# Weight splits, idle matmuls and one right operand of the up projection: a layer's first stage re-ordered, and the third operand's low part made by a DMA

## The chip, the core and the metric

The kernel runs on one NeuronCore of one Trainium2 chip. The metric is the device time of one execution in microseconds. An execution that is profiled leaves a page and a trace; others are only timed. The engines are called as in the profile: PE (TensorE matmuls), PEld (its weight loads), DVE (VectorE), ACT (ScalarE), POOL (GpSimd), SP (SyncE, which here only issues DMAs). PE, DVE and ACT each run their instructions strictly in order.

## The reference

One layer of a hybrid trunk for 1024 tokens and 1024 channels, in float32:

```python
h = rms_norm(x, g_mix)
z = einsum("bsd,de->bse", h, w_in) + b_in        # 1024 x 1024 by 1024 x 7168
va, ga, xb, gb, sa, sb = split(z)
# conv branch of va, ga; RG-LRU branch of xb, gb; both gated and merged to m
x = x + einsum("bsd,de->bse", m, w_o)
h = rms_norm(x, g_mlp)
f = square(relu(einsum("bsd,df->bsf", h, w_1)))  # the up projection, 1024 x 4096
x = x + einsum("bsf,fd->bsd", f, w_2)
return rms_norm(x, g_final)
```

## The kernel before, in words

**Products.** Every float32 operand is split into a high part, rounded to the type that PE multiplies in one pass, and a low part, the rest. A product is the sum of three matmuls: high by high, high by low and low by high. The high part is a copy by ScalarE. The low part is made in one of two ways: `low` (L703) and `split` (L51) subtract the high part from the source on VectorE; `split_dma` (L64 to L68) has ScalarE copy the source with its sign turned (L66), and a DMA issued by POOL adds the source onto that copy (L67, `accum_op=ALU.add`); the high part follows (L68). In the names of tiles, `h` and `l` at the end stand for high and low.

**First stage.** The tokens are taken in two halves of 512. Row sums of squares come from `x_square` (L186), alternating between VectorE and ScalarE in the first half and on ScalarE in the second. `x_root` (L199) makes of them 1/rms by a square root on ScalarE and Newton's step on VectorE (L95 to L105), and puts it on four diagonals (L208 by VectorE, L210 by ScalarE). `x_spread` (L212) multiplies these by a matrix of ones (L217), so that every partition holds the factor of every token: the PSUM tile `rb`. `x_scaled` (L219) multiplies a column block c of the transposed x by it on VectorE (L221) and takes the high part `xh` on ScalarE (L222); `x_low` (L224) takes the low part `xl` on VectorE (L226). There are eight column blocks. They meet the first three column chunks of `w_in` (`N0 = 3`, PSUM tiles z16 to z18). `first_w` (L233) splits a chunk's weight by `split_dma`; `first_z` (L242, matmuls on L245) does its high part by `xh` and `xl`; `late_z` (L248, L250) its low part by `xh`. `half` (L315) lays out one half of the tokens: for each c the scaling of block c, whatever `beside` adds, the low part of block c-1, and the matmuls that this allows; a chunk joins at the c in `joins`. Ahead of the first products stand idle matmuls (`idle_mm`, L303 to L305): ones by the identity, 16 and then 6, whose result nobody reads. They write the second half of the tile `rb`. All this stands in a block `manual_schedule` (L292), in which the order of PE, DVE and ACT is that of the text; POOL and SP, and the rest of the kernel outside such blocks, are ordered by a scheduler that estimates times. From the fourth chunk on, `zchunk` (L353) does each chunk with `mm3` (matmuls on L92).

**DMAs of the first stage.** SP loads, in this order: four row tiles of x, weight 0, two pieces of the transposed x, weight 1, a piece, weight 2, a piece, four more row tiles, four pieces of the second half, then the weights of later chunks.

**Up projection.** h by w_1 is done in blocks of two by two, by a scheme with seven products p = 1 to 7 instead of eight, for each of 16 tiles i of two chunks of 128 columns. `h2_sum` (L733) makes the right operands (sums of blocks `hq` in `ht`; for p = 3 the block itself), `h2_part` and `h2_parts` (L711, L743) split them into `b{p}h` and `b{p}l` with `low`. `up_load` loads a tile's weights, `up_lhs` (L762) makes the left operand o of (i, p): sums `s` on VectorE (L773 to L777), the high part on ScalarE (L785), the low part on VectorE (L704). `up_step` (L805) does 12 matmuls (`up_mm`, L794) and reads them off. Four PSUM banks a, b, c, d serve a tile: p = 1, 2 write a, 6 writes b, 5 and then 3 write c, 7 and then 4 write d. The sum of p = 5 is read from c by VectorE (L821) before p = 3 goes on in the same bank, likewise d (L823) between p = 7 and p = 4. L819 reads b. In the traces the banks of tile 0 are f0a to f0d.

The first four tiles (`AHEAD = 4`) are done in part while the right operands are still being made. That is a second block `manual_schedule` (L880 to L920); behind it a loop (L1011) does the rest of the list `seq`, which holds (0, 6), (0, 5), (0, 7), (0, 3), (0, 4), (1, 6) and so on. It prepares left operands `look = 5` steps ahead, before the step's matmuls. In the block stand, at the end: the left operand of (0, 7), the steps (0, 6) and (0, 5), both halves of the right operands 3 and 4 with `h2_parts`, and the left operands of (0, 3) and (0, 4). The step (0, 7) is the loop's first.

Of the kernel before, what the change touches and what calls it, by code (L numbers as in the profile page):

```python
# [9 lines left out]
F32 = mybir.dt.float32  # L10
F32R = mybir.dt.float32r
# [21 lines left out]
def trunk_kernel(ctx: ExitStack, tc: tile.TileContext, x, xt_in, vecs, w_in, w_a_out, w_b_out,  # L33
# [145 lines left out]
    for t in range(4, 8):  # L179
        load_x(t)  # L180

# [17 lines left out]
    def x_root(hf):  # L199

        ss, v, s, t, r = (rs_x[hf][:, i, :] for i in range(5))
        nc.vector.tensor_scalar(v, ss, 1.0 / D, EPS, ALU.mult, ALU.add)
        newton_rstd(r, v, s, t)
        rb["d"] = rd = T(f"rd{hf}")
        for i in range(4):
            d = rd[:, i * P:(i + 1) * P]
            if i % 2 == 0:
                nc.vector.tensor_scalar(d, ident, r[:, i:i + 1], None, ALU.mult)  # L208
            else:
                nc.scalar.activation(d, ident, AF.Copy, scale=r[:, i:i + 1])  # L210
# [22 lines left out]
    def first_w(i):  # L233
        if i < 2:
            wh, wl = split_w(raw0[i], [P, 8, P], f"w{i}")
        else:
            wh, wl = (T(f"w{i}_{n}", F32R).rearrange("p (k c) -> p k c", c=P) for n in "hl")
            split_dma(raw0[i], wh, wl)
        w0.append((wh, wl))
        z0.append(PS(f"z{16 + i}"))  # L240

    def first_z(i, hf, ks):  # L242
        for k in ks:
            for n, a in enumerate((xh, xl)):
                nc.tensor.matmul(z0[i][:, HALVES[hf]], w0[i][0][:, k, :], a[k][:, HALVES[hf]],  # L245
                                 start=k == 0 and n == 0, stop=False)

    def late_z(i, hf, ks=range(8)):  # L248
        for k in ks:
            nc.tensor.matmul(z0[i][:, HALVES[hf]], w0[i][1][:, k, :], xh[k][:, HALVES[hf]],  # L250
                             start=False, stop=k == 7)
# [40 lines left out]
    with tc.manual_schedule(engines={mybir.EngineType.Activation, mybir.EngineType.DVE,  # L292
# [7 lines left out]
        rb["tile"] = PS("rb", "ps2")  # L300
        nc.tensor.matmul(rb["tile"][:, 0:1], ones, rs_x[0][:, 0, 1:2], start=True, stop=True)

        def idle_mm(n):  # L303
            for _ in range(n):
                nc.tensor.matmul(rb["tile"][:, HS:HS + P], ones, ident, start=True, stop=True)  # L305

        idle_mm(16)
        x_root(0)
        x_spread(0)
        idle_mm(6)  # L310
        first_w(0)
        for c2 in range(4):
            load_xc(1, c2)

        def half(hf, beside, joins):  # L315


            seen = [0] * N0
            for c in range(9):
                if c < 8:  # L320
                    x_scaled(hf, c)
                beside(c)
                if c:
                    x_low(hf, c - 1)
                    for i in range(N0):
                        if c >= joins[i]:
                            first_z(i, hf, range(seen[i], c))
# [12 lines left out]
        late_z(1, 0)  # L340
        x_spread(1)
        late_z(2, 0)
        half(1, lambda c: None, (1, 1, 1))
        late_z(1, 1)
        late_z(2, 1)
# [400 lines left out]

    NP = DFF // P // 2
# [132 lines left out]
    with tc.manual_schedule(engines={mybir.EngineType.Activation, mybir.EngineType.DVE,  # L880
# [31 lines left out]
        h2_sum(3, 1)  # L912
        up_step(0, 6, up_ps)
        h2_parts(3)
# [4 lines left out]
        h2_parts(4)  # L919
        up_lhs(0, 4)  # L920
    KC = 2
# [90 lines left out]
    for n in range(2 * AHEAD + 2, len(seq)):  # L1012
# [251 lines left out]
```

## Time and profile before

| what | value |
|---|---|
| median of 3 timed runs | 1625.59 us (1624.93 to 1626.24) |
| the profiled execution: time, span of its trace | 1623.46 us, 1621.6 us |
| PE busy | 1601.3 us, 99% of the span |
| PE waits, first stage, on its first products | 1.50, 0.22, 0.53 and 0.30 us |
| PE waits, up projection, 1024 to 1034 us | 0.10, 0.80 and 1.13 us |
| granted clock of TensorE | 1.00, but 0.50 from 18.6 to 25.4 us |

Times in the views are microseconds from the first instruction of the trace. A row of a timeline gives start, duration, engine, line, operation, output and inputs by the program's names with shapes, the number of instructions merged into the row, and in brackets the engine's idle time before it with the line that ended it. Matmuls overlap, so that a row's duration (0.39 us) is longer than the distance from one to the next; a PE that shows as busy is not on that account at its peak. The rows of the view of stretches give busy time and count of PE, PEld, DVE, ACT and POOL, then the clock (1.00 is full), the mean busy share of the 16 DMA engines and what they moved in GB/s. "To landing" is the time from a DMA's issue to its last byte.

### The profile page before, as it was taken

To read this page: it belongs to the slowest core of one execution; us is meant where nothing else is said; L and a number is where in the kernel's file an instruction comes from. 1 tells how busy PE (TensorE), PEld (TensorE's weight loads), DVE (VectorE), ACT (ScalarE), POOL (GpSimd) and SP (SyncE) were. 2 spreads that over 40 slices of the span, in tenths; PEclk is the share of its full clock that TensorE was granted. 3 is DMA by queue.
4 is the path that set the end of the run, shared out by engine and by line. 5 is a ranking of instruction groups with operands and counts; after the bars stand their busy time and mean duration, and the time that the engine had idled before them with its cause. 6 is when DMAs were issued, how large, how long until landed. Compare 5 with 4: busy or idle time off the path is not lost.

```text
span 1621.6 us, 18723 instructions
## 1 busy us (share of the span) xinstructions
PE 1601.3 (99%) x7070; PEld 1314.9 (81%) x7070; DVE 1094.7 (68%) x1319; ACT 931.2 (57%) x1185; POOL 179.8 (11%) x244
## 2 busy tenths in 40 slices
PE   7999999999999999999999999999999999999997
PEld 6888888888888888888788888788888888888886
DVE  4699999998989836611412146965555457888898
ACT  5579898999972347722522335654444466555552
POOL 1111111111210100010211100000000001111110
PEclk9999999999999999999999999999999999999999
DMA  9456676667755544464755641433322579889862
GB/s 317 100 116 159 133 152 147 158 146 167 173 129 127 131 98 97 91 201 98 172 146 123 182 156 65 171 116 116 117 104 104 184 231 233 213 216 228 213 130 104
DMA packets 81513, 245.90 MB, mean 152 GB/s; under 512 B 9568, under 2 KB 11104, under 8 KB 81424
## 3 DMA queue, kind: packets, MB, share of 16 engines
q0 software_dynamic: 29392, 97.24, 29.6%
q1 hardware_dynamic: 51888, 147.22, 27.5%
q8 instruction: 55, 0.90, 0.2%
q14 instruction: 34, 0.28, 0.1%
q10 hardware_dynamic: 144, 0.26, 0.0%
HBM read 123.05 MB, written 33.55 MB: 97 GB/s over the span
## 4 chain that ended last, share of the span: by engine, by line
PE 96%; DVE 1%; ACT 1%; issue 1%; DMA 0%; SPq 0%; DVEq 0%; ACTq 0%
PE z L92 35%; PE d L1048 14%; PE yb L92 8%; PE ya L92 5%; PE o L656 3%; PE e L1163 2%; PE keep L1048 2%; PE o L92 2%; PE z L245 1%; PE rg L419 1%; PE rg L421 1%; PE rg L420 1%; PE o L680 1%; PE z L250 1%; PE tr_m L728 0%
## 5 line engine op out<-in xcount | busy, mean ns | idle before, releaser
L492 DVE SCALAR_TENSOR_TENSOR y<-u,vec,y 128x1024 f32<-128x1024 f32 x240 | 307.2, 1280 | 15.8 <-ACT y L488 10.7
L92 PE MATMUL z<-xh,win_h 128*128 128x512 f32 x848 | 262.8, 391 | 0.0
L92 PE MATMUL z<-xl,win_h 128*128 128x512 f32 x848 | 261.8, 390 | 0.0
L92 PE MATMUL z<-xh,win_l 128*128 128x512 f32 x848 | 200.9, 389 | 0.0
L92 PEld LDWEIGHTS z<-xh,win_h 128*128 128x128 f32 x848 | 159.3, 188 | 35.8 <-issue 1.7
L92 PEld LDWEIGHTS z<-xl,win_h 128*128 128x128 f32 x848 | 159.2, 188 | 33.7 <-issue 0.2
L92 PEld LDWEIGHTS z<-xh,win_l 128*128 128x128 f32 x848 | 159.2, 188 | 33.0
L1060 DVE TENSOR_TENSOR acc<-acc,d 128x1024 f32<-128x1024 f32 x72 | 87.8, 1219 | 33.3 <-PE d L1048 32.6
L68 ACT ACTIVATE win_h<-win_raw 128x1024 fp32r<-128x1024 f32 x53 | 55.9, 1056 | 89.7 <-PE z L92 79.3
L67 POOL DMA_DIRECT2D win_l<-win_raw x53 | 46.6, 880 | 338.8 <-ACT win_l L66 313.1
L66 ACT ACTIVATE win_l<-win_raw 128x1024 fp32r<-128x1024 f32 x53 | 55.5, 1050 | 5.7 <-PE z L92 5.7
L619 DVE TENSOR_TENSOR sb<-yb,sb 128x1024 f32<-128x1024 f32 x8 | 9.8, 1224 | 72.3 <-PE yb L92 72.3
L785 ACT ACTIVATE o<-s 128x512 fp32r<-128x512 f32 x64 | 38.1, 621 | 34.7 <-DVE s L777 29.6
L595 DVE TENSOR_TENSOR m<-ya,sa 128x1024 f32<-128x1024 f32 x8 | 9.8, 1225 | 68.8 <-PE ya L92 68.8
L785 ACT ACTIVATE o<-w_raw 128x512 fp32r<-128x512 f32 x40 | 25.0, 624 | 50.9 <-DVE o L704 50.8
L574 DVE TENSOR_TENSOR v<-v,ge 128x512 f32<-128x512 f32 x24 | 16.4, 689 | 47.7 <-ACT ge L572 47.7
L381 DVE SCALAR_TENSOR_TENSOR v<-xb,vec,v 128x1023 f32<-128x1023 f32 (+2 forms) x36 | 45.3, 1271 | 1.2 <-ACT v L376 1.1
L67 POOL DMA_DIRECT2D db_1l<-wr x7 | 6.1, 872 | 356.9 <-ACT db_1l L66 334.4
L688 DVE TENSOR_TENSOR x<-xr,o 128x1024 f32<-128x1024 f32 x8 | 9.6, 1219 | 51.9 <-PE o L656 37.7
L704 DVE TENSOR_TENSOR o<-s,o 128x512 fp32r<-128x512 f32 x64 | 42.5, 684 | 2.9 <-ACT o L785 2.8
L118 ACT ACTIVATE xn<-x 128x1024 f32<-128x1024 f32 x8 | 8.4, 1057 | 58.5 <-DVE x L688 53.4
L92 PE MATMUL ya<-suh,wa_h 128*128 128x512 f32 x128 | 39.4, 389 | 0.0
(1101 smaller groups left out, 3859.0 us busy)
## 6 DMA issues: line engine op xcount, KB each, us to landing
win_raw<-in_w_in_dram SPq DMA_DIRECT2D x53, 512.0 KB, 4.5
win_l<-win_raw POOLq DMA_DIRECT2D x53, 512.0 KB, 4.6
fr<-fd SPq DMA_DIRECT2D x32, 512.0 KB, 5.2
wr<-in_w_dram SPq DMA_DIRECT2D x32, 512.0 KB, 5.9
w_raw<-in_w_dram SPq DMA_DIRECT2D x31, 512.0 KB, 3.4
gates<-s POOLq DMA_DIRECT2D x32, 256.0 KB, 4.3
fd<-fa SPq DMA_DIRECT2D x16, 512.0 KB, 3.1
fd<-fb SPq DMA_DIRECT2D x16, 512.0 KB, 3.0
```

The lines of the kernel that those rows point to most:

```text
L66: nc.scalar.activation(l, src, AF.Copy, scale=-1.0)
L67: nc.gpsimd.dma_start(l, src, accum_op=ALU.add)
L68: nc.scalar.activation(h, src, AF.Copy)
L92: nc.tensor.matmul(ps[:, HALVES[hf]], a, b[hf], start=i == 0, stop=i == len(todo) - 1)
L381: nc.vector.scalar_tensor_tensor(v[:, d:S], a[:, 0:S - d], cbw_c[:, w * 12 + t:w * 12 + t + 1], v[:, d:S], ALU.mult, ALU.add)
L492: nc.vector.scalar_tensor_tensor(acc, u[:, w:w + S], caw[:, w * 8 + j:w * 8 + j + 1], acc, ALU.mult, ALU.add)
L656: nc.tensor.matmul(ps[:, HALVES[hf]], tok(a, k, t), wo[k][b][:, HALVES[hf]], start=k == 0 and b == 0 and n == 0, stop=k == 7 and b == 1)
L704: tt(l, src, h.bitcast(F32), ALU.subtract)
L785: nc.scalar.activation(o[:, 0], src, AF.Copy)
L1048: nc.tensor.matmul(o, a, b, start=n == 0 and (p != 1 or g == 0), stop=n == len(todo) - 1, skip_group_check=p == 1 and g > 0)
L1060: tt(acc[p, q2], acc[p, q2], ps, ALU.add)
L1163: nc.tensor.matmul(o, a, b, start=n == 0, stop=n == len(todo) - 1)
```

## The change

In the first stage:

- The idle matmuls write a PSUM tile `spare` of their own instead of the second half of `rb`.
- `first_w` comes in parts. The high part of weight 0 is copied by ScalarE inside `x_root(0)`, ahead of the diagonals. The low parts of weights 0 and 1 are subtracted by VectorE; weight 2 keeps the copy with turned sign and the accumulating DMA. The low part of weight 0 stands ahead of the first scaling, that of weight 1 ahead of the low part of column block 2.
- Chunk 0 takes its three products of a column block at once, high by low in between, with one idle matmul before and one after the product with the first low part. Chunks 1 and 2 join one column block earlier; their products of the weight's low part stay at the end of a half.
- The four loads of the second half's transposed x are written further up.

In the up projection:

- Right operand 3 is split by `split_dma` instead of by VectorE, ahead of the step (0, 6).
- The step (0, 7) comes into the hand-ordered block, ahead of the subtraction for the second half of right operand 4; the left operand of (0, 4) comes between the two halves of right operand 4.

```diff
+    for c2 in range(4):
+        load_xc(1, c2)
...
-    def x_root(hf):
+    def x_root(hf, beside=lambda: None):
...
         newton_rstd(r, v, s, t)
+        beside()
...
-    def first_w(i):
+    def first_w(i, part):
+        if part == "h":
...
+            nc.scalar.activation(wh, raw0[i], AF.Copy)
+        elif part == "l":
+            nc.vector.tensor_tensor(w0[i][1], raw0[i], w0[i][0].bitcast(F32), ALU.subtract)
         else:
-            split_dma(raw0[i], wh, wl)
+            nc.scalar.activation(w0[i][1], raw0[i], AF.Copy, scale=-1.0)
+            nc.gpsimd.dma_start(w0[i][1], raw0[i], accum_op=ALU.add)
...
+        spare = PS("spare")
...
-                nc.tensor.matmul(rb["tile"][:, HS:HS + P], ones, ident, start=True, stop=True)
+                nc.tensor.matmul(spare[:, 0:P], ones, ident, start=True, stop=True)
         idle_mm(16)
-        x_root(0)
+        x_root(0, lambda: first_w(0, "h"))
+        rb["tile"] = PS("rb", "ps2")
         x_spread(0)
+        first_w(0, "l")
         idle_mm(6)
-        first_w(0)
...
                 if c:
+                    first_z(0, hf, c - 1, "hh")
+                    first_z(0, hf, c - 1, "lh")
+                    if c in idle:
+                        idle_mm(idle[c])
                     x_low(hf, c - 1)
-                    for i in range(N0):
-                        if c >= joins[i]:
-                            first_z(i, hf, range(seen[i], c))
-                            seen[i] = c
-                    if c > 4:
-                        late_z(0, hf, (2 * c - 10, 2 * c - 9))
+                    first_z(0, hf, c - 1, "hl")
+                    for i in range(1, N0):
+                        while joins[i] <= c and seen[i] < c:
+                            first_z(i, hf, seen[i], "hh")
+                            first_z(i, hf, seen[i], "hl")
+                            seen[i] += 1
+                    if c in idle:
+                        idle_mm(idle[c])
         def beside(c):
             if c in (1, 2):
-                first_w(c)
-            elif 4 < c < 9:
+                first_w(c, "h")
+            elif c == 3:
+                first_w(1, "l")
+                first_w(2, "dma")
+            if 4 < c < 9:
                 x_square(c - 1, nc.scalar)
-        half(0, beside, (1, 3, 4))
+        half(0, beside, (1, 2, 3), {1: 1})
...
+    def h2_parts_dma(p):
+        for c2 in range(2):
+            bh[p][c2], bl[p][c2] = T(f"b{p}h{c2}", F32R), T(f"b{p}l{c2}", F32R)
+            split_dma(ht[p, c2], bh[p][c2], bl[p][c2])
...
         h2_sum(3, 1)
+        h2_parts_dma(3)
         up_step(0, 6, up_ps)
-        h2_parts(3)
         up_lhs(0, 3)
         up_step(0, 5, up_ps)
         for c2 in range(2):
             h2_sum(4, c2)
-        h2_parts(4)
+        h2_part(4, 0, ht[4, 0])
         up_lhs(0, 4)
+        bh[4][1], bl[4][1] = T("b4h1", F32R), T("b4l1", F32R)
+        nc.scalar.activation(bh[4][1], ht[4, 1], AF.Copy)
+        up_step(0, 7, up_ps)
+        low(bl[4][1], ht[4, 1], bh[4][1])
...
-    for n in range(2 * AHEAD + 2, len(seq)):
+    for n in range(2 * AHEAD + 3, len(seq)):
```

More of the change, by code (lines that the diff above doesn't have):

```diff
@@ L298, in trunk_kernel, with half @@
             x_square(t, (nc.vector, nc.scalar)[t % 2])
-        rb["tile"] = PS("rb", "ps2")
-        nc.tensor.matmul(rb["tile"][:, 0:1], ones, rs_x[0][:, 0, 1:2], start=True, stop=True)
+        spare = PS("spare")
+        nc.tensor.matmul(spare[:, 0:1], ones, rs_x[0][:, 0, 1:2], start=True, stop=True)
         def idle_mm(n):
             for _ in range(n):
-                nc.tensor.matmul(rb["tile"][:, HS:HS + P], ones, ident, start=True, stop=True)
+                nc.tensor.matmul(spare[:, 0:P], ones, ident, start=True, stop=True)
         idle_mm(16)
-        x_root(0)
+        x_root(0, lambda: first_w(0, "h"))
+        rb["tile"] = PS("rb", "ps2")
         x_spread(0)
+        first_w(0, "l")
         idle_mm(6)
-        first_w(0)
-        for c2 in range(4):
-            load_xc(1, c2)
-        def half(hf, beside, joins):
+        def half(hf, beside, joins, idle):
             seen = [0] * N0
```

39 lines of the change are left out of this document (20 added, 19 removed).

## The prediction

> **What bounds the kernel now.** From the page I take the span:
>
> ```profile
> span 1621.6 us, 18723 instructions
> ```
>
> Next I read the view of stretches: busy time and count of PE, PEld, DVE, ACT, POOL, then the granted clock of TensorE and the DMA share.
>
> ```profile
> 17.00:57.00 40.00, 38.77 (x157) 30.56 (x158) 28.48 (x85) 23.76 (x36) 3.17 (x4) 0.91 0.56 175
> 57.00:980.00 923.00, 922.92 (x4066) 754.63 (x4065) 604.44 (x651) 567.74 (x699) 130.38 (x178) 1.00 0.58 141
> 1024.00:1034.00 10.00, 7.97 (x33) 5.67 (x32) 9.90 (x14) 5.37 (x7) 0.00 (x0) 1.00 0.23 75
> 1034.00:1500.00 466.00, 466.00 (x2058) 385.54 (x2057) 311.35 (x373) 246.79 (x307) 29.62 (x34) 1.00 0.59 173
> ```
>
> TensorE is the bound: 922.92 of 923 us from 57 us on, 466 of 466 from 1034 on. What PE gains or loses before 57 us, or between 1024 and 1034 us, therefore reaches the end one for one. Those are the two places of the change. In the first the clock is also down (0.91 over 40 us); in the second VectorE is the full engine (9.90 of 10) and PE waits.
>
> The timelines come next, one engine at a time: start, duration, line, operation; in brackets the idle time before it and who ended it. ScalarE and PE around the first row scaling:
>
> ```profile
> 12.61 0.69 ACT L210 ACTIVATE rd<-ident,stx 128x128 f32<-128x128 f32 x2 [1.10 <-DVE stx L105]
> 13.21 1.04 ACT L66 ACTIVATE w_l<-w_raw 128x1024 fp32r<-128x1024 f32 x1
> 14.15 1.04 ACT L68 ACTIVATE w_h<-w_raw 128x1024 fp32r<-128x1024 f32 x1
> 16.34 0.63 ACT L222 ACTIVATE xh<-xc 128x512 fp32r<-128x512 f32 x1 [1.15 <-DVE xc L221]
> ```
> ```profile
> 13.12 1.06 PE L217 MATMUL rb<-rd,ones 128*128 128x128 f32 x8
> 14.02 1.50 PE L305 MATMUL rb<-ident,ones 128*128 128x128 f32 x12
> 17.02 0.50 PE L245 MATMUL z<-xh,w_h 128*128 128x512 f32 x1 [1.50 <-ACT xh L222]
> ```
>
> VectorE in the same stretch:
>
> ```profile
> 15.56 1.41 DVE L221 SCALAR_TENSOR_TENSOR xc<-xc,vec,rb 128x512 f32<-128x512 f32 x2 [2.46 <-PE rb L305]
> 17.00 0.69 DVE L226 TENSOR_TENSOR xl<-xc,xh 128x512 fp32r<-128x512 f32 x1
> 17.61 0.74 DVE L221 SCALAR_TENSOR_TENSOR xc<-xc,vec,rb 128x512 f32<-128x512 f32 x1
> 18.27 0.68 DVE L226 TENSOR_TENSOR xl<-xc,xh 128x512 fp32r<-128x512 f32 x1
> ```
>
> What the reader is to see: the first scaling waits 2.46 us for L305, the idle matmuls, and not for L217, the broadcast whose result it reads. They share a tile. PE then stands still for 1.50 us. The clock answers:
>
> ```profile
> 15.20:18.60 3.40, 1.56 (x6) 0.61 (x5) 3.00 (x5) 2.23 (x4) 0.25 (x1) 1.00 1.02 348
> 18.60:22.00 3.40, 2.69 (x5) 1.57 (x6) 2.36 (x4) 3.40 (x5) 1.59 (x2) 0.50 1.03 287
> 1029.00:1032.40 3.40, 2.06 (x8) 1.42 (x9) 3.33 (x6) 1.74 (x3) 0.00 (x0) 1.00 0.24 94
> ```
>
> After a stretch with 6 PE records in 3.4 us the clock halves; with 8 records in 3.4 us, in the up projection, it stays at 1.00.
>
> **The change, first stage.** The idle matmuls write a tile of their own, so the first scaling waits for the broadcast alone. What that takes is seen in the second half, where nothing lies between:
>
> ```profile
> 34.20 2.43 PE L250 MATMUL z<-xh,w_l 128*128 128x512 f32 x10
> 36.47 1.05 PE L217 MATMUL rb<-rd,ones 128*128 128x128 f32 x8
> ```
> ```profile
> 37.56 1.41 DVE L221 SCALAR_TENSOR_TENSOR xc<-xc,vec,rb 128x512 f32<-128x512 f32 x2 [2.70 <-PE rb L217]
> ```
>
> 37.56 - 36.47 = 1.09 us, so the first scaling goes from 15.56 to 13.12 + 1.09 = 14.21, 1.35 us earlier. Two weight pieces are put in the way, and both fit. The high part (1.04, as L68) goes ahead of the diagonals on ScalarE, where 1.10 us are idle before 12.61; its data are there:
>
> ```profile
> 2.59 0.52 SPq L61 DMA_DIRECT2D w_raw<-in_w_in_dram  x1
> ```
> ```profile
> w_raw<-in_w_in_dram SPq DMA_DIRECT2D x1, 512.0 KB, 8.6
> ```
>
> 2.59 + 8.6 = 11.2, ahead of 11.5 where ScalarE falls idle. The low part is a new subtraction on VectorE, 1.14 us a step (a pair of the same shape takes 2.35, below); VectorE's diagonals feed the broadcast at 13.12, so it starts at about 13.05 and ends its step at 14.2. If the weight landed later, ScalarE's diagonals and all behind them would slip by the same amount.
>
> From there I step the three engines through the new order with the rows' own steps: scaling 0.66 and low part 0.61 (17.00 to 17.61 to 18.27), high part 0.78 after its scaling (15.56 to 16.34), matmul (36.47 - 34.20)/10 = 0.227. High part 0 starts at 14.99 and ends at 15.61; PE leaves the idle matmuls at 15.4 and starts the first product at 15.7 instead of 17.02. Seven slots follow (two of them new idle matmuls, 0.45 us). The product with low part 1 waits 0.3 us. Then VectorE does the low part of weight 1 (1.14) ahead of low part 2, which starts at 19.35 and ends at 20.03: PE waits 0.7 us and goes on at 20.08, with 12 of the 144 products behind it (3 chunks, 3 products, 8 columns, 2 halves). From here a column feeds 7 products, 1.59 us, and costs VectorE 1.27: PE does not wait again, apart from some 0.3 us at the change of halves. The rest is 132 x 0.227 = 29.9, plus the broadcast 0.80, plus 0.4 for waits and refilling after them: 51.2. Before:
>
> ```profile
> 55.97 0.62 PE L92 MATMUL z<-xh,win_h 128*128 128x512 f32 x2
> ```
>
> **Term 1: 55.97 - 51.2 = 4.8 us earlier.** The same stepping of the old order, with half clock where it was seen, gives 56.0. About 1.3 us of the term is the start, 1.2 us is the clock (the old order at full clock ends at 54.7), the rest is waits.
>
> This needs the clock to stay up. Between 15.2 and 18.6 the new order issues 11 products and idle matmuls (many of the latter in two records), in the next 3.4 us about 11: more than the 8 that kept it. That the x pieces are there for scalings up to 1.35 us earlier I take from the row at 15.56, which waited for PE and not for its DMA. The loads of the second half's x stand earlier in the text, but in the same place of SP's queue, and with two of three accumulating DMAs gone they land earlier. The one that stays, for weight 2, is needed at 32.8; it is issued at 20.6 and these took at most 11.1 us, so it lands by 31.7:
>
> ```profile
> DMA to landing us min/median/max: 8.9/9.4/11.1
> ```
>
> The chunk behind needs its high part at 51.2; ScalarE's new order (a low copy and the evacuation ahead of it) gives it at about 49.7.
>
> [...]
>
> **The change, up projection.** ScalarE, VectorE and PE there:
>
> ```profile
> 1020.39 1.99 ACT L713 ACTIVATE b3h<-hq 128x1024 fp32r<-128x1024 f32 x2
> 1022.29 0.61 ACT L785 ACTIVATE o<-s 128x512 fp32r<-128x512 f32 x1
> ```
> ```profile
> 1021.73 2.35 DVE L704 TENSOR_TENSOR b3l<-hq,b3h 128x1024 fp32r<-128x1024 f32 x2
> 1024.00 0.68 DVE L704 TENSOR_TENSOR o<-s,o 128x512 fp32r<-128x512 f32 x1
> 1024.60 0.68 DVE L821 TENSOR_TENSOR fa<-f0c,u 128x512 f32<-128x512 f32 x1
> ...
> 1030.34 0.68 DVE L704 TENSOR_TENSOR o<-w_raw,o 128x512 fp32r<-128x512 f32 x1
> 1030.94 0.68 DVE L773 TENSOR_TENSOR s<-w_raw 128x512 f32<-128x512 f32 x1
> ```
> ```profile
> 1029.21 0.50 PE L794 MATMUL f0d<-b4h,o 128*128 128x512 f32 x1 [0.80 <-ACT o L785]
> ...
> 1031.07 0.73 PE L794 MATMUL f0d<-b4h,o 128*128 128x512 f32 x2 [1.13 <-DVE o L704]
> ...
> 1034.15 0.39 PE L794 MATMUL f1b<-b6h,o 128*128 128x512 f32 x1
> ```
>
> VectorE loses the pair of 2.35 us. ScalarE gains two copies at 0.95 a step, ahead of its copy for the third left operand: that one goes from 1022.29 to 1024.19 and ends at 1024.8. VectorE is strictly in order, and its next instruction is that operand's low part: it stands idle from 1021.7 to 1024.85, longer than what it saved. Behind it waits the evacuation of f0c, 1025.45 instead of 1024.60, on which the next product of f0c (p = 3) waits. Then on VectorE: two sums to 1028.3, one low part of b4, the left low part of p = 4 at 1029.53, the evacuation of f0d at 1030.13, the second low part, and the sums of the next tile at 1031.87 instead of 1030.94. PE takes up f0d at 1030.9 (before 1029.21, but with its third product at 1031.07) and runs it without a stop to 1033.7; the next tile's third product of f1b waits for its low part until 1034.72, after 1034.15 before, and one product of f1c which used to be done by then is not; refilling costs 0.1. The later evacuation of f0d also holds back the square of fa, its store at the head of SP's queue and the six weight loads behind that, by some 1.8 us; tile 2 reads them only some 7 us later on VectorE, so I cost that at nothing.
>
> **Term 2: 0.57 + 0.23 + 0.1 = 0.9 us later.** Bounds: at best all of PE's waiting from 1024 to 1034 goes, 2.0 us earlier; the other end is the third rival.
>
> The accumulates themselves are hidden. They start at 1021.7 and 1023.6, and at the usual
>
> ```profile
> win_l<-win_raw POOLq DMA_DIRECT2D x53, 512.0 KB, 4.6
> ```
>
> they land at 1026.3 and 1028.2; PE wants them at 1026.5 and 1027.9, and f0d cannot start before 1030.9 anyway, which covers a landing up to 1029.6.
>
> **Sum.** -4.8 + 0.9 = -3.9 us. The profiled execution took 1623.5 us (span 1621.6) and would take 1619.6. It lies 2.1 us under the median of the runs, 1625.6; the median would come to 1621.7.
>
> **Rivals.** *The clock falls all the same.* PE still waits four times before 20.1 us. A half-rate stretch as before, 18.60 to 25.4, costs at most 6.8/2 = 3.4 us less the waits it hides, about 3.2. For: it fell here once. Against: the counts above. Time 1625.6 - 1.6 + 0.9 = 1624.9.
>
> *The second edit pays.* If ScalarE got its left operand out before the b3 copies, VectorE would run 2.35 us ahead and the waits of 2.0 us would go: 1625.6 - 4.8 - 2.0 = 1618.8. Against: the order of instructions on ScalarE puts all four copies first.
>
> *The accumulates land late, and the kernel is slower.* In the up projection the last one gates p = 3 from the eighth product on. Landing after 1029.6, each microsecond costs one; with the 11.1 us of the first stage it lands at 1034.7, PE does 17 products (3.9) after it and reaches the next tile at 1038.7 where it was at 1033.47: 5.4 later with the f1c product, against 4.8 won: 1626.2. It decides from 1034.1 on, and by over 0.2% from 1037.4, 13.8 us after its start. Against: from 1024 to 1034 the DMA share is 0.23, in the first stage it was 1.02.
> [...]
>
> **How the numbers follow.** A measurement tells about 0.2% from no change, 3.25 us. The sum as worked out: 0.70; its own range is 1620.6 to 1622.9, and some 0.56 of it is over 3.25 us. Clock falls: 0.13, within 0.2%. Second edit pays: 0.07, faster. Late landing, and whatever I overlook on that side: 0.10, of which 0.07 is slower by over 0.2%. Faster 0.63, same 0.30, slower 0.07. The range takes in the clock's case above and the start of the second rival below: 1619.6 to 1625.2.
>
> **What would show it.** Term 1: first scaling near 14.2, no row of clock below 1.00 between 18 and 26 us, one wait of some 0.7 us ended by VectorE's low part near 20, the first product of the fourth chunk near 51.2. Term 2, all 4.8 us earlier by then: VectorE idle about 3 us ahead of the left low part, f0c resuming 1.0 us after f0d's first round, PE's idle time in those ten microseconds a little more than before. I am wrong if the clock halves, if p = 3 waits for a DMA by more than 0.4 us, or if PE waits anew behind 57 us.

## The result, and the profile after

The changed kernel takes **1623.20 us** (median of 22 executions, 1622.08 to 1624.32) against 1626.09 us (22 executions, 1624.07 to 1628.03) for the kernel before, measured beside it: ratio 0.9982, 95% interval 0.9976 to 0.9989, 2.9 us less. The forecast was 3.9 us less (1621.7). The two profiled executions differ by only 0.75 us: 1623.46 us before, 1622.71 after. Both gaps have to be explained: 2.9 instead of 3.9 by the medians, and 0.9 (of span) by the profiles.

The span, from the page after, and the view of stretches after, with the same stretches as those shown of before (busy time and count of PE, PEld, DVE, ACT, POOL; clock; DMA share; GB/s):

```profile
span 1620.7 us, 18731 instructions
```
```profile
15.20:18.60 3.40, 3.16 (x18) 2.30 (x17) 3.36 (x7) 3.26 (x5) 0.00 (x0) 1.00 1.03 411
18.60:22.00 3.40, 2.89 (x13) 2.06 (x12) 3.40 (x5) 2.52 (x4) 0.89 (x1) 1.00 1.02 406
17.00:57.00 40.00, 39.41 (x176) 31.84 (x176) 32.44 (x92) 25.21 (x37) 2.93 (x5) 1.00 0.56 174
...
980.00:1000.00 20.00, 18.59 (x99) 15.65 (x98) 10.42 (x21) 9.58 (x20) 0.53 (x1) 1.00 0.33 111
1024.00:1034.00 10.00, 8.18 (x31) 5.58 (x32) 9.90 (x14) 5.39 (x8) 0.00 (x0) 1.00 0.52 129
1034.00:1500.00 466.00, 466.00 (x2057) 385.43 (x2056) 310.16 (x371) 247.78 (x308) 29.58 (x34) 1.00 0.59 173
```

The clock is 1.00 throughout these stretches of the first stage (0.50 before, from 18.6 to 25.4). But PE is not full between 980 and 1000 us (18.59 of 20), where it used to be, and from 1024 to 1034 it waits about as long as before (8.18 busy of 10, before 7.97). The stretch of before that takes in 980 to 1000 us:

```profile
980.00:1024.00 44.00, 44.00 (x212) 37.00 (x211) 31.78 (x45) 25.51 (x42) 1.06 (x2) 1.00 0.24 84
```

PE's timeline after, first stage and start of the fourth chunk:

```profile
13.44 1.06 PE L220 MATMUL rb<-rd,ones 128*128 128x128 f32 x8
14.33 1.50 PE L310 MATMUL spare<-ident,ones 128*128 128x128 f32 x12
16.00 0.50 PE L254 MATMUL z<-xh,w_h 128*128 128x512 f32 x1 [0.17 <-ACT xh L225]
...
20.38 0.50 PE L254 MATMUL z<-xl,w_h 128*128 128x512 f32 x1 [0.51 <-DVE xl L229]
...
51.61 0.61 PE L92 MATMUL z<-xh,win_h 128*128 128x512 f32 x2
```

VectorE's first scaling after:

```profile
14.53 1.41 DVE L224 SCALAR_TENSOR_TENSOR xc<-xc,vec,rb 128x512 f32<-128x512 f32 x2 [1.08 <-PE rb L220]
```

The wait of the first scaling is now for the broadcast (L220) and not for the idle matmuls. The fourth chunk starts at 51.61 instead of 55.97: 4.36 us won. How much of it is left further on (differences of the unrounded times):

| first matmul of | before, us | after, us | difference |
|---|---|---|---|
| fourth chunk (L92) | 55.97 | 51.61 | -4.36 |
| mu (its product with ones) | 591.09 | 587.45 | -3.65 |
| f0a | 991.73 | 989.63 | -2.10 |
| f2a | 1006.12 | 1004.16 | -1.97 |
| f1d | 1038.91 | 1037.93 | -0.98 |
| e (near the end) | 1569.42 | 1568.50 | -0.92 |

So 0.7 us is lost between 52 and 587 us, 1.7 at the first products of the up projection, 1.0 in its middle, and nothing behind it. PE's timeline after, at those places:

```profile
989.63 0.47 PE L815 MATMUL f0a<-b1h,o 128*128 128x512 f32 x1 [1.41 <-DVE x L704]
...
1024.31 0.47 PE L815 MATMUL f0c<-b3h,o 128*128 128x512 f32 x1 [0.95 <-DVE fa L842]
...
1027.13 0.50 PE L815 MATMUL f0c<-b3l,o 128*128 128x512 f32 x1 [0.97 <-DMA b3l<-hq]
...
1028.99 0.47 PE L815 MATMUL f0d<-b4h,o 128*128 128x512 f32 x1 [0.43 <-DVE fa L844]
...
1032.81 0.73 PE L815 MATMUL f1b<-b6h,o 128*128 128x512 f32 x2
```

The wait of 1.41 us at f0a is new: it is for x, the last residual sum of VectorE (L704). In the kernel before PE did not wait there, though that sum was no earlier. Its PE and VectorE:

```profile
991.73 0.39 PE L794 MATMUL f0a<-b1h,o 128*128 128x512 f32 x1
```
```profile
991.93 1.22 DVE L688 TENSOR_TENSOR x<-xr,o 128x1024 f32<-128x1024 f32 x1 [4.31 <-PE o L680]
```

f0a began 0.20 us before the sum did. So f0a doesn't need the sum's result; something else has come to tie them.

### The profile page after: what moved, and what is told of

Same layout as the page of the kernel before. It is cut to its first block, busy times and chain, and to the rows that moved or that the text cites. A ratio compares the mean times of both kernels' runs of the same rounds, so it can differ in the third digit from the quotient of the medians.

```text
span 1620.7 us, 18731 instructions
## 1 busy us (share of the span) xinstructions
PE 1600.2 (99%) x7074; PEld 1313.3 (81%) x7074; DVE 1094.9 (68%) x1319; ACT 931.0 (57%) x1185; POOL 179.8 (11%) x244
## 4 chain that ended last, share of the span: by engine, by line
PE 94%; issue 2%; DVE 2%; ACT 1%; DMA 1%; POOL 0%; SPq 0%; POOLq 0%; DVEq 0%; ACTq 0%
PE z L92 33%; PE d L1073 14%; PE yb L92 8%; PE ya L92 5%; PE o L672 3%; PE e L1188 2%; PE keep L1073 2%; PE o L92 2%; PE z L254 2%; PE rg L437 1%; PE rg L435 1%; DMA vl<-v 1%; PE rg L436 1%; PE o L696 1%; PE tr_m L744 0%
## 5 line engine op out<-in xcount | busy, mean ns | idle before, releaser
L92 PE MATMUL z<-xh,win_h 128*128 128x512 f32 x848 | 262.9, 391 | 0.0
L92 PE MATMUL z<-xl,win_h 128*128 128x512 f32 x848 | 261.8, 390 | 0.0
L92 PE MATMUL z<-xh,win_l 128*128 128x512 f32 x848 | 200.9, 389 | 0.0
L92 PEld LDWEIGHTS z<-xh,win_h 128*128 128x128 f32 x848 | 159.2, 188 | 35.8 <-issue 1.7
L92 PEld LDWEIGHTS z<-xl,win_h 128*128 128x128 f32 x848 | 159.2, 188 | 33.8 <-issue 0.2
L92 PEld LDWEIGHTS z<-xh,win_l 128*128 128x128 f32 x848 | 159.2, 188 | 33.0
L704 DVE TENSOR_TENSOR x<-xr,o 128x1024 f32<-128x1024 f32 x8 | 9.6, 1218 | 51.9 <-PE o L672 37.7
L92 PE MATMUL ya<-suh,wa_h 128*128 128x512 f32 x128 | 39.4, 389 | 0.0
```

Of the source, the lines that this page charges most:

```text
L92: nc.tensor.matmul(ps[:, HALVES[hf]], a, b[hf], start=i == 0, stop=i == len(todo) - 1)
```

## Theories and experiments

Theory: the first stage won what the forecast says; the wait at f0a is a clash over PSUM that the new tile `spare` brings; the second edit costs 1.0 us; and the medians differ by more than the profiles since the clock falls somewhere else in most executions of before. Rivals: the wait at f0a comes just because PE is earlier; the second edit pays or costs nothing; the first stage's gain is given back wherever PE gets ahead. All ratios are to the kernel before, run beside the experiment on the same chip, with 95% intervals.

### e1, e2: each part alone

e1 is the changed kernel with the old up projection; e2 is the old kernel with the new one. The diff is that of e1 against the changed kernel; e2 against before is the same with the signs turned:

```diff
-        h2_parts_dma(3)
         up_step(0, 6, up_ps)
+        h2_parts(3)
...
-        h2_part(4, 0, ht[4, 0])
+        h2_parts(4)
         up_lhs(0, 4)
...
-        up_step(0, 7, up_ps)
...
-    for n in range(2 * AHEAD + 3, len(seq)):
+    for n in range(2 * AHEAD + 2, len(seq)):
```

> The first-stage part of the change alone; the up projection as before. Theory: by the two traces the up projection's part costs 1.0 us, so this kernel is 1.0 us under the changed one, about 1622.2 us. PE waits 1.4 us at the first product of f0a as the changed kernel does, since this part brings the extra PSUM tile. In the up projection the row of f1d lies where it lay before the change, less the shift at f0a. Rival (the up projection's part costs nothing, or pays): 1623.2 us or more. Rival (the first stage gains nothing that lasts): 1626 us.

> The up projection's part alone on the first stage of before. Theory: 1.0 us more than before, 1627.1 us: PE waits about 1.0 us for VectorE ahead of p = 3 and about 1.0 us in the middle of p = 3 for the accumulating DMA, and the wait ahead of f0d is shorter. There is no wait at the first product of f0a. Rival (the edit pays, and loses only because the changed kernel arrives there at another time): 1624 to 1626 us, with no wait for the DMA.

Measured: e1 1623.36 us, 0.9982 (0.9974 to 0.9991); e2 1626.08 us, 1.0002 (0.9993 to 1.0011). By the medians the second edit costs nothing: both theories (1622.2 and 1627.1 us) missed, and the rival of e1 has the number. By the traces it costs what the theories said, and the wait for the DMA that the rival of e2 left out is there: in e2 f0d starts 0.68 us ahead of before and f1d 0.32 behind it, 1.0 us lost, with these two waits of PE:

```profile
1025.59 0.47 PE L799 MATMUL f0c<-b3h,o 128*128 128x512 f32 x1 [0.94 <-DVE fa L826]
...
1028.59 0.50 PE L799 MATMUL f0c<-b3l,o 128*128 128x512 f32 x1 [1.05 <-DMA b3l<-hq]
```

In e1 the wait of 1.41 us at f0a is there, in e2 it isn't. What differs between trace and median is the clock, as far as its mean tells. Of the 33 executions of before beside e1 and e2, 22 had a mean clock of 0.995, 6 had 0.996 and 5 had 0.997; of the 11 of e2 none was below 0.996. In e1, 5 of 11 had 0.997, and their median was 1624.1 us against 1621.8 for the other six; in the changed kernel all 22 had 0.998 or 0.999. So the second edit brings waits and, by the mean clock, takes away a fall of it; where that fall lies is looked at under e7.

### e3, e4: two more turns of the PSUM buffers

```diff
+    for n in range(2):
+        PS(f"turn{n}")
     for t, ps in enumerate(o_first()):
```

e3 is the changed kernel with these lines, e4 is e1 with them.

> The changed kernel with two PSUM tiles more, which nobody writes or reads, taken from the same three buffers ahead of the output projection, so that its tiles lie in the buffers in which they lay before the change. Theory (the extra tile of the idle matmuls turned the rotation, and the first bank of the up projection now falls on the bank that the last residual still reads): the wait at f0a is gone, and the time is 1.6 us less than that of the changed kernel, 1621.6 us. Rival (PE is simply ahead of VectorE there since the first stage is shorter): the wait stays, 1623.2 us.

> The first-stage part alone with the two PSUM tiles more. Theory: both losses are gone, 1.0 + 1.6 us less than the changed kernel, 1620.6 us, 5.5 us less than before. Rival (the gain of the first stage is given back later, wherever that is): 1622 to 1623 us.

Measured: e3 1623.13 us, 0.9982 (0.9974 to 0.9991), e4 1622.15 us, 0.9980 (0.9972 to 0.9989). The wait stays. PE in e3:

```profile
989.03 0.47 PE L815 MATMUL f0a<-b1h,o 128*128 128x512 f32 x1 [1.41 <-DVE x L704]
```

Both expectations missed, but the theory was not tested: the edit had not moved anything, since two tiles that nobody writes take no turn. The addresses in the built kernels, first PSUM bank of each tile (a tile of the output projection has two banks, f0a one):

```
kernel            first tile    last o tile (o7)    f0a
before            rb      0     4                   0
changed, e1, e3   spare   0     0                   0
```

Before, rb is the first PSUM tile asked for, and its pool entry ("ps2", one buffer) gets banks 0 and 1. In the changed kernel `spare` is first, and "ps", from which the o tiles come, gets them. Then f0a, in bank 0 of the next pool, would have to wait until VectorE has read o7 out of the same bank, which would be the 1.41 us. e5 tests it.

With their addresses unchanged, e3 and e4 are in effect the changed kernel and e1 once more. Taken together, the 33 executions with the second edit (changed kernel, e3) have a median of 1623.2 us and the 32 without it (e1, e4, and e12 below) 1622.5: over these the edit costs 0.7 us, less than the 1.0 of the traces.

### e5: rb asked for first

```diff
+        rb["tile"] = PS("rb", "ps2")
         spare = PS("spare")
...
-        rb["tile"] = PS("rb", "ps2")
         x_spread(0)
```

> The changed kernel with one line moved: the tile rb is asked for ahead of the tile of the idle matmuls, so that rb has the PSUM banks 0 and 1 again, as in the kernel before, and the last tile of the output projection lies in the banks 2 and 3 instead of 0 and 1, where the first bank of the up projection is. Theory (the order of first use gave the banks away): the wait of 1.4 us at the first product of f0a is gone, 1.6 us less than the changed kernel, 1621.6 us. Rival (PE is simply ahead of VectorE there): the wait stays, 1623.2 us.

Measured: 1621.15 us, 0.9970 (0.9958 to 0.9982), in 6 executions. In its build o7 lies in banks 2 and 3 and f0a in bank 0. The wait is gone, although PE comes earlier still:

```profile
987.81 0.39 PE L815 MATMUL f0a<-b1h,o 128*128 128x512 f32 x1
```

Its gain from mu (-3.84) to f2a (-3.92) is kept, where the changed kernel lost 1.7 us. So it was not that PE is simply ahead of VectorE. The order in which two tiles are first asked for cost 1.7 us by the traces and 2 by the medians, at a place 970 us behind the edit.

### e7, e12: where the clock falls

e7 is the kernel before unchanged, e12 is e1 unchanged, each for another profile.

> The kernel before, unchanged, for another profile. In the runs so far the executions of before with a mean clock of 0.995 are longer than those with 0.996 or 0.997. Theory (the clock also falls in the up projection, in some executions, where PE waits 2 us out of 10): in a profile with 0.995 there is a second stretch at 0.50 near 1030 us, beside that near 20 us, and the landmarks from f1d on are later than those before it. Rival: the stretch in the first stage is longer, 13.6 us, and nothing happens at 1030 us.

> The first-stage part alone once more, for another profile: in its first run 5 of 11 executions had a mean clock of 0.997 and were some 2 us longer than those with 0.998 or 0.999; the profiled one was not among them. Theory (in these the clock falls in the up projection, as it did in the second profile of before): if the profiled execution has 0.997, it shows a stretch at 0.50 near 1030 us and none in the first stage. Rival: the stretch lies near 20 us, or near 989 us behind the wait at f0a. If the profiled execution has 0.998 or more, it tells nothing new, and where the clock fell in the others stays open.

e7 was profiled at 1627.49 us, with a mean clock of 0.996 (not 0.995). Its stretches:

```profile
17.12:20.53 3.41, 1.74 (x4) 0.67 (x4) 3.37 (x6) 3.17 (x5) 0.66 (x1) 1.00 1.02 280
1030.88:1034.29 3.41, 1.62 (x6) 1.06 (x7) 3.38 (x5) 2.20 (x4) 0.00 (x0) 1.00 0.10 40
1034.29:1037.70 3.41, 3.41 (x10) 2.67 (x9) 3.35 (x6) 1.48 (x3) 0.00 (x0) 0.50 1.00 318
```

The second stretch of the theory is there: besides the fall from 20.53 to 27.36 the clock is at 0.50 from 1034.29 to 1037.70, right behind the waits at f0d. That the executions at 0.995 have such a fall too is read from their mean clock; none of them was profiled. f0d is 2.34 us later than in the first profile of before and f1d 3.97: the fall costs 1.6 us here. e12 (1623.24 us, 0.9983, 0.9974 to 0.9993) was profiled at a mean clock of 0.999 and shows no fall, so where it lies in the 0.997 executions of e1 was not seen. Its emptiest stretch, behind which the clock stayed at 1.00:

```profile
1026.92:1030.33 3.41, 1.79 (x7) 0.86 (x5) 3.41 (x5) 3.31 (x5) 0.00 (x0) 1.00 0.00 0
```

In the traces with a fall the changes of the clock lie 3.41 us or a multiple of it apart (before: 18.60 and 25.43; e2: 17.46 and 24.29; e6: 1032.70 and 1039.52; e7: 13.70, 20.53, 27.36, 1034.29 and 1037.70). The stretches above are cut on that grid, and so are these, of e2, of the changed kernel and of e6 (below):

```profile
14.05:17.46 3.41, 1.68 (x12) 1.18 (x11) 2.31 (x4) 1.81 (x4) 0.53 (x1) 1.00 1.02 377
17.46:20.87 3.41, 2.96 (x5) 1.30 (x6) 2.94 (x5) 3.41 (x5) 0.91 (x2) 0.50 1.04 271
```
```profile
1022.69:1026.10 3.41, 2.46 (x10) 1.44 (x9) 3.23 (x4) 0.92 (x2) 0.00 (x0) 1.00 1.02 192
1026.10:1029.51 3.41, 2.00 (x8) 1.35 (x8) 3.41 (x5) 2.38 (x4) 0.00 (x0) 1.00 0.11 19
```
```profile
1029.28:1032.70 3.42, 0.95 (x5) 0.42 (x3) 0.89 (x2) 0.00 (x0) 0.00 (x0) 1.00 0.95 384
1032.70:1036.11 3.41, 2.13 (x5) 1.71 (x6) 3.34 (x6) 1.31 (x3) 0.00 (x0) 0.50 1.03 422
```

In the 14 traces the clock fell, once it had come up and ahead of the last matmuls, behind five stretches of the grid: PE was busy in them for 0.95 us of 3.41 (e6), 1.56 (before, 15.20 to 18.60), 1.62 and 1.74 (e7) and 1.68 (e2). The emptiest stretch behind which it stayed at 1.00 is that of e12, with 1.79. The count of records does not go with it: behind 12 of them the clock fell in e2, behind 7 it stayed in e12. PE's two waits in the up projection of before lie close together, and the emptiest 3.41 us there, 1027.68 to 1031.09, have it busy for 1.48 us; in the changed kernel its waits lie further apart, and the emptiest, 1023.36 to 1026.77, have 1.85. In the first profile of before the grid happened to divide the two waits (2.02 us busy from 1028.95 to 1032.36), and the clock stayed at 1.00. Of the 85 executions of before that ran beside the experiments 54 read 0.995; how many of them have the fall in the up projection is not shown. Of all executions with the new first stage, 9 of 37 with the old up projection had a mean clock of 0.997, and none of 46 with the new one (e1, e4, e11, e12 against the changed kernel, e3, e5, e10).

### e8, e10: what in the first stage holds the clock

e8 is the kernel before with the idle matmuls on their own tile; e10 is e5 without the two new idle matmuls among the products.

```diff
+        spare = PS("spare")
...
-                nc.tensor.matmul(rb["tile"][:, HS:HS + P], ones, ident, start=True, stop=True)
+                nc.tensor.matmul(spare[:, 0:P], ones, ident, start=True, stop=True)
```
```diff
-        half(0, beside, (1, 2, 3), {1: 1})
+        half(0, beside, (1, 2, 3), {})
```

> The kernel before with one edit: the idle matmuls write a tile of their own, which is asked for after rb. Theory: the first scaling waits for the broadcast alone and starts about 1.1 us behind its first matmul, 1.3 us earlier than before; if the clock falls as before, 1624.6 us. If the wait that is gone was what made the clock fall, it stays at 1.00 in the first stage and 1623.4 us follow. Rival (ScalarE, which splits weight 0 at that time, is the limit): the first product starts no more than 0.3 us earlier, 1625.5 us.

> The run with rb first, without the two idle matmuls between the products of column block 0. Theory of the prediction (the clock stays up because PE issues enough records in each window; 8 in 3.4 us keep it): with the two left out there are still about 9 products from 15.2 to 18.6 us, the clock stays at 1.00 and the time is the same within 0.5 us, 1621 us; the wait at the first low part is 0.4 us longer. Rival (the two idle matmuls hold the clock): a stretch at 0.50 from about 18 to 25 us, mean clock 0.996 to 0.997 in most executions, 1624 us.

Measured: e8 1624.25 us, 0.9988 (0.9979 to 0.9996); e10 1621.11 us, 0.9974 (0.9963 to 0.9985), the same as e5. PE in e8:

```profile
12.57 1.06 PE L217 MATMUL rb<-rd,ones 128*128 128x128 f32 x8
...
15.13 0.49 PE L245 MATMUL z<-xh,w_h 128*128 128x512 f32 x1 [0.16 <-ACT xh L222]
...
34.54 1.16 PE L217 MATMUL rb<-rd,ones 128*128 128x128 f32 x8 [1.34 <-DVE rd L208]
...
54.16 0.62 PE L92 MATMUL z<-xh,win_h 128*128 128x512 f32 x2
```

From the broadcast to the first product it takes 2.56 us (before 3.90): 1.34 us from the separate tile. The clock stays at 1.00 in the profiled execution too: in the two stretches of the grid from 13.91 to 20.74 PE is busy 2.50 and 2.60 us. But 54.16 is only 1.8 us ahead of before, and 0.55 of that is the broadcast, which happens to come earlier here (12.57 against 13.12). The other 1.26 us are what tile and clock leave: with the old order PE still waits for VectorE in the first half, and stands 1.34 us at the second broadcast. The median lies between the two numbers of the theory. The new order of the products and weight parts is worth another 3.4 us: in e3, whose broadcast comes at 12.61, the fourth chunk starts at 50.81. The two new idle matmuls hold nothing: without them PE is busy 2.95 and 2.91 us of 3.41 in the two stretches from 14.29 to 21.12, and the mean clock was 0.998 or 0.999 in all 7 executions.

### e6, e9: the accumulating DMA early

Both are e5 with another layout of the second edit. The two copies with turned sign and their DMAs go to a place where ScalarE was idle for 2.2 us; the left operand of (0, 3) goes ahead of the two high parts. e6 also reads f0d ahead of operand 4's low parts; e9 leaves that where the change has it.

```diff
             h2_sum(7, c2)
+        for c2 in range(2):
+            h2_sum(3, c2)
+            bl[3][c2] = T(f"b3l{c2}", F32R)
+            nc.scalar.activation(bl[3][c2], ht[3, c2], AF.Copy, scale=-1.0)
+            nc.gpsimd.dma_start(bl[3][c2], ht[3, c2], accum_op=ALU.add)
         up_load(0, (1,))
...
-        h2_parts_dma(3)
         up_step(0, 6, up_ps)
         up_lhs(0, 3)
+        for c2 in range(2):
+            bh[3][c2] = T(f"b3h{c2}", F32R)
+            nc.scalar.activation(bh[3][c2], ht[3, c2], AF.Copy)
```

And in e6 alone:

```diff
+        up_step(0, 7, up_ps)
         h2_part(4, 0, ht[4, 0])
         up_lhs(0, 4)
-        bh[4][1], bl[4][1] = T("b4h1", F32R), T("b4l1", F32R)
-        nc.scalar.activation(bh[4][1], ht[4, 1], AF.Copy)
-        up_step(0, 7, up_ps)
-        low(bl[4][1], ht[4, 1], bh[4][1])
+        h2_part(4, 1, ht[4, 1])
```

> As the run with rb first, and the up projection's part laid out anew: the two copies with turned sign and the two accumulating DMAs for right operand 3 stand ahead of the left operand of (0, 6), where ScalarE is idle for 2.2 us; the left operand of (0, 3) stands ahead of the two high parts; the reading of f0d stands ahead of the low parts of operand 4. Theory (the edit loses since ScalarE does four copies ahead of the left operand and the DMA starts late): the accumulates land by 1018 us, p = 3 starts right behind p = 7, PE's waits between 1022 and 1034 us fall from 2.5 to about 0.9 us, 2.5 us less than the run with rb first, about 1619 us. Rival (VectorE's own work or the DMA is the limit there): the waits move to f0d and f1b and the time stays within 0.5 us of the run with rb first.

Measured: 1625.41 us, 0.9999 (0.9991 to 1.0008). A miss. The waits at p = 3 are gone, but PE and VectorE stand at the next tile:

```profile
1033.97 0.80 PE L815 MATMUL f1b<-b6h,o 128*128 128x512 f32 x1 [3.74 <-ACT o L806]
```
```profile
1031.78 0.69 DVE L794 TENSOR_TENSOR s<-w_raw 128x512 f32<-128x512 f32 x1 [3.04 <-DMA w_raw<-in_w_dram]
```

Reading f0d early makes the store of fa due early, and the scheduler put it ahead of the two loads of tile 1's weights in SP's queue: these were issued from 1025.3 us on instead of from 1010 to 1013 as in e5. SP's queue in e6:

```profile
1024.83 0.33 SPq L868 DMA_DIRECT2D fd<-fa  x1
1025.27 10.94 SPq L778 DMA_DIRECT2D w_raw<-in_w_dram  x8
```

During PE's idling the clock fell too (the stretches of e6 above: 0.95 us busy, then 0.50 from 1032.70 on), and the mean clock was 0.996 or 0.997 in all 11 executions, against 0.998 or 0.999 in those of e5 and e9.

> The run with the early DMA, with two steps put back: the copies of operand 4 and the left operand of (0, 4) stand ahead of the reading of f0d again, so that the store of fa falls behind the two weight loads of tile 1 in SP's queue. Theory (the run before lost only since those loads had come behind the store, and VectorE waited for the weights): PE's wait of 3.7 us at f1b is gone, p = 3 and p = 4 run with less than 0.3 us of waiting, f1b waits about 0.5 us for its left operand, the clock stays at 1.00, and the time is 2.4 us less than that of the run with rb first, 1618.8 us. Rival (the early DMA or the changed order costs elsewhere): 1621 us or more.

Measured: **1618.03 us**, 0.9953 (0.9940 to 0.9965). PE in e9:

```profile
1022.62 0.39 PE L815 MATMUL f0c<-b3h,o 128*128 128x512 f32 x1
...
1025.63 0.47 PE L815 MATMUL f0d<-b4h,o 128*128 128x512 f32 x1
...
1028.72 0.50 PE L815 MATMUL f1b<-b6h,o 128*128 128x512 f32 x1
```

The theory holds (1618.8 forecast): p = 3 follows p = 7 without a wait, and f1b starts 8.82 us behind the first product of f0d (at 1019.90), in e5 11.60 us behind it. It is the fastest kernel of the study, 7.4 us under before and some 5 under the changed kernel.

### e11: only the first stage, with rb first

e1 with the edit of e5:

```diff
+        rb["tile"] = PS("rb", "ps2")
         spare = PS("spare")
...
-        h2_parts_dma(3)
         up_step(0, 6, up_ps)
+        h2_parts(3)
```

> The run with rb first, with the up projection as before the change: only the first-stage part. Theory (the up projection's part costs 1.0 us in waits, but keeps the clock up, which else falls there in some executions): executions of two kinds, with a mean clock of 0.998 to 0.999 about 1.0 us shorter than those of the run with rb first, and, in some 3 to 5 of 11, with 0.997, about 1 to 2 us longer; the median within 1 us of that run's, 1620.5 to 1622 us, with a wider spread. Rival (the up projection's part costs 1.0 us, and nothing else): 1620.1 us, with the spread of the run with rb first.

Measured: 1619.99 us, 0.9965 (0.9951 to 0.9978); all 5 executions at 0.998 or 0.999. That is the rival's number. But with a mean clock of 0.997 in 9 of the other 32 executions of this sort, five without it are no great surprise ((23/32)^5 is 0.19), so the theory is not refuted by it. From f0d to f1d e11 gains 0.99 us on e5 in the traces: the second edit's waits once more. By the intervals e5 and e11 can't be told apart.

## Why the prediction was right, and where not

- **What bounds the kernel: right.** PE's time at the two places reached the end one for one, except where PE met a new wait.
- **Term 1, first stage: right in mechanism and nearly in size.** Forecast 4.8 us, measured 4.36. The first scaling came 14.53 - 13.44 = 1.09 us behind the broadcast, as worked out; the wait near 20 us is 0.51 (forecast 0.7), the clock stayed up. The missing 0.4 us is mostly the start: the forecast put the broadcast at 13.12 as before, and it came at 13.44. It is not the diagonals that set that time (their copy by ScalarE began at 11.83) but the 16 idle matmuls ahead of it, and these run at half rate at first: PE has 23 records in the 4.7 us from 7.5 us on, and 26 in the 2.6 us from 12.4 on. Counted from the broadcast the gain is 4.68 us. Its parts are not those of the forecast, which gave 1.3 us to the start and 1.2 to the clock: with the tile alone both together leave 1.26 (e8), and the new order brings 3.4.
- **The argument for the clock: right outcome, wrong reason.** The count of records does not tell when the clock falls: it fell behind 12 in 3.41 us, with PE busy for 1.68 us (e2), and not behind 7, with 1.79 (e12). The two idle matmuls that were counted in do nothing (e10: the same time, clock at 0.998 or 0.999).
- **Term 2, up projection: right, but for the landing.** Forecast 0.9 us later, measured 0.99. VectorE stands idle ahead of the left low part for 3.02 us, as forecast (the row is under the rivals). Shifted by the 1.97 us that PE was ahead, f0d starts at 1030.96 (forecast 1030.9) and the third product of f1b at 1034.78 (forecast 1034.72). The second accumulate landed 5.4 us after its start and not 4.6, so PE waited 0.97 us in p = 3, more than the 0.4 named as a sign of being wrong. It cost nothing: it lies inside the time that f0d had to wait for VectorE anyway, the cover of 1.4 us that the forecast worked out. The sign was badly chosen, since a wait that takes another's place is no loss.
- **"PE waits anew behind 57 us": this failed.** The forecast took the gain of 4.8 us as kept to the end. The tile `spare`, looked at only for what waits on it, changed who owns banks 0 and 1, and PE lost 1.7 us at f0a (e5 shows it). A further 0.7 us went in small waits on accumulating DMAs of `vl` between 84 and 587 us, which every kernel with the short first stage shows (0.4 to 2.2 us more than the first profile of before). The kernel before shows them too, in its other profile (0.9 us in e7). So it is not shown that the short first stage brings them; no experiment took them away, and their cause stays open. PE's timeline in e4, then in e7:

```profile
171.22 0.48 PE L437 MATMUL rg<-vl,rgh 96*96 96x512 f32 x1 [0.58 <-DMA vl<-v]
```
```profile
399.00 0.47 PE L421 MATMUL rg<-vl,rgh 96*96 96x512 f32 x1 [0.23 <-DMA vl<-v]
```

- **From the profile to the median: this failed too, on the other side.** The forecast took its two terms, worked out in one execution, off the median. That execution of before lies 2.6 us under its median; most others have a lower mean clock (54 of the 85 beside the experiments 0.995, the profiled one 0.996), which is read as a second fall in the up projection (seen in e7) that the second edit removes (no 0.995 in e2). By the profiles the change gains 4.36 - 0.7 - 1.7 - 1.0 = 0.9 us; by the medians 2.0 more. How much of the 2.0 is the fall is not shown: beside e1 the five executions of before at 0.997 have a median of 1624.5 us against 1625.8 of all 33, which makes some 1.3 us, an estimate.
- **The rivals.** POOL's and VectorE's timelines after, for the third:

```profile
1019.77 0.88 POOL L67 DMA_DIRECT2D b3l<-hq  x1 [29.46 <-ACT b3l L66]
1021.66 0.89 POOL L67 DMA_DIRECT2D b3l<-hq  x1 [1.01 <-ACT b3l L66]
```
```profile
1022.87 0.69 DVE L720 TENSOR_TENSOR o<-s,o 128x512 fp32r<-128x512 f32 x1 [3.02 <-ACT o L806]
```

  The clock did not fall, so the first is out. The second, that the edit pays if the left operand gets out ahead of the copies, is wrong for this change and right as a remark on it: e9 does that, with the DMA early, and gains 2.8 us on e5 between f0d and f1d. The third priced the landing well, but it came 0.5 us inside its cover. POOL's two issues took 0.88 and 0.89 us, as long as the mean of the 53 accumulates of weights (880 ns), so the 0.8 us by which the second landed later do not lie in its issue.
- **The chances.** The forecast counted a change of under 0.2%, 3.25 us, as no change, and gave 0.30 to that and 0.63 to a clear gain. The 2.9 us fall under the less likely of the two, though the interval leaves out no change at all. No run shows the spread of term 1 that the forecast's own range, 1620.6 to 1622.9, takes in: the 22 executions of the changed kernel lie between 1622.08 and 1624.32 us, with a median 0.3 us above that range.

That the total came out near the forecast is in part luck: two terms that were not in it, 2.4 us lost and 2.0 us won, nearly cancel.

## What to carry to other kernels

Before a new PSUM tile is added, look at which banks each pool entry gets and who reads them last: here the bill came 970 us later, and it was one line to mend. Add up short waits of PE that lie close together instead of judging them one by one: in e7 the clock fell behind 3.41 us in which the waits at f0d left PE busy for 1.62, and in the changed kernel, with three waits of 0.95, 0.97 and 0.43 us spread out and PE busy for 2.00 in the emptiest of the stretches above, it did not. A DMA that took over an engine's work was better issued early here (2.8 us between e5 and e9), and when steps are moved, what changes places in a shared load queue has to be read from that queue (in e6 two loads went out from 1025.3 us on instead of 1010 to 1013).

## What the runs showed of the hardware

The time at which the clock first comes up differs between two executions of one kernel (10.33 and 13.16 us in e1 and e12), and the start moves with it. PE's 16 idle matmuls begin between 7.25 and 7.56 us in every trace. The views give 1.00 ahead of the first change of the clock, but PE's pace there is about half: in e1 it has 14 records in the 2.7 us from 7.5 on, and 26 in the 2.7 us from 10.4 on; in e12 13, then 15, and 28 in the 2.8 us from 13.2 on. e1 and e12 are the same kernel; PE in e1, then in e12:

```profile
7.45 5.18 PE L310 MATMUL spare<-ident,ones 128*128 128x128 f32 x32
12.47 1.06 PE L220 MATMUL rb<-rd,ones 128*128 128x128 f32 x8
```
```profile
7.54 6.50 PE L310 MATMUL spare<-ident,ones 128*128 128x128 f32 x32
13.87 1.06 PE L220 MATMUL rb<-rd,ones 128*128 128x128 f32 x8
```

The clock comes up at 10.33 us in e1 and at 13.16 in e12, and the same 16 idle matmuls take 5.18 and 6.50 us; the broadcast, in order behind them, is 1.4 us later. In the 14 traces it came up between 10.33 (e1) and 13.70 us (e7), a spread of 3.4 us. By an estimate from these rows, 1.4 us at the broadcast, that can be a good part of the 2.1 us by which the spans of e1 and e12 differ (1619.1 and 1621.2 us). Fewer idle matmuls might leave the start to the diagonals, which ScalarE begins between 11.6 and 12.6 us; that was not tried.

When the clock came up shows on the same grid. At the start PE was busy for 3.30 us in the stretch that ends at 10.33 in e1, and the clock came up; in e7 it was busy for 3.19 us in the one that ends at 10.29, and the clock came up one stretch later, at 13.70 (the 16 idle matmuls took 6.76 us there, 5.18 in e1). After a fall, PE's busy time in each stretch at 0.50, up to the return to 1.00:

| fall | busy of 3.41 us at 0.50 | back at 1.00, us |
|---|---|---|
| e2, 17.46 us | 2.96, 3.41 | 24.29 |
| before, 18.60 us | 2.71, 3.41 | 25.43 |
| e7, 20.53 us | 2.86, 3.41 | 27.36 |
| e6, 1032.70 us | 2.13, 3.41 | 1039.52 |
| e7, 1034.29 us | 3.41 | 1037.70 |

So the falls near 20 us and that of e6 lasted 6.83 us, and that of e7 in the up projection, with PE busy throughout, 3.41.
